# Background steps, a decay clamp and VectorE's order in a two-block network on one Trainium2 core

## The chip, the cores and the metric

The kernel runs on one core of one Trainium2 chip. Its time is the device time in microseconds (us) of one execution. The time before is the median of three runs, 1569.42 us (1568.95 to 1573.41). The engines are TensorE (PE: matmuls, and its weight loads PEld), VectorE (DVE), ScalarE (ACT), GpSimd (POOL) and SyncE (SP), which issues most transfers.

## The reference

Two layers of two blocks work on 256 positions of width 1024. Block 1 adds the output of two mixers, a state-space one (SSD) and a dilated attention, and then a gated feed-forward; block 2 is a retention mixer, a block attention (MoBA) and a gated embedding. Each part begins with an RMS norm. What matters here:

```python
def rms_norm(x, w):
    xf = x.astype(jnp.float32)
    y = xf * lax.rsqrt(jnp.mean(xf * xf, axis=-1, keepdims=True) + RMS_EPS)
    return (y * w.astype(jnp.float32)).astype(x.dtype)
...
def ssd_mixer(z, xbc, dt_raw, conv_w, conv_b, dt_bias, a_log, d_skip, norm_w):
    ...
    dt = jax.nn.softplus(dt_raw.astype(f32) + dt_bias.astype(f32))
    a = -jnp.exp(a_log.astype(f32))
    ...
def ssd_chunked(xh, dt, a, bm, cm):
    ...
    a_cum = jnp.cumsum(a_dt, axis=-1)
    causal = jnp.tril(jnp.ones((SSD_CHUNK, SSD_CHUNK), dtype=bool))
    decay = jnp.exp(jnp.where(causal, a_cum[..., :, None] - a_cum[..., None, :], -jnp.inf))
    cb = jnp.einsum("bclgn,bcsgn->bgcls", cc, bc)
    y_diag = jnp.einsum("bgecls,bcsgep->bclgep", cb[:, :, None] * decay, x)
    decay_states = jnp.exp(a_cum[..., -1:] - a_cum).transpose(0, 3, 4, 1, 2)
```

`dt` are the step sizes, `a_cum` their cumulative sums times a decay rate. The exponent of `decay` is at most 0 below the diagonal; above it the kernel clamps it at 0 and multiplies by a mask later.

## The kernel before

**Weights.** Every large product is made in three passes, high times high, high times low and low times high part. The weights come as 1 MB pieces `raw` on SP's queue; ScalarE casts the high part `wh` (L156), VectorE subtracts it for the low part `wl` (L159), and while `pool_every` is 4 (the bc projections and the SSD groups) GpSimd makes every fourth `wl`. A unit is 128x1024 weights: 24 matmuls with 256 columns (L451 to L453, or L435 to L437), or 12 with 512 (L398 to L400) in the slabs. `split_to` (L143) keeps the casts two units ahead of PE, in three buffers each.

**Background steps.** `tick` (L344) runs once per unit. It advances the first generator of each queue in `self.bg` to its next `yield`. So one `yield` more in a generator puts all that follows in it one unit later. `drain` runs a queue to its end. The queues of `block1` (L704) are `qn` (norm pieces), `qa` (attention), `qs` (SSD groups) and `qt` (group tails).

**Order.** The order of instructions on each engine is set by a scheduler from a timeline of its own, except between `ordered(True)` and `ordered(False)` (L843), where it is the order of the program, for all engines or for those named.

**Block 1.** First the norm and the values of both attention halves, then queries and keys of half 0, queries and keys of half 1 with half 0's `attention` (L498) in the background, then `dt_path` (L546), at once and in one piece, then the bc projections; after the first pair of these, half 1's `attention` goes to `qa`. Each of its four heads takes scores, a softmax (GpSimd adds the three patterns, L526; VectorE scales by L527 and L528), transposes of `E` on PE (L387) and the product with the values.

Then come four groups of 8 heads: the `xs` projection with its convolution (L612 to L617: a ScalarE and three VectorE instructions per tile, then a half-size SiLU, L616 and L617), `z`, and a gate or a branch. `ssd_group` (L619) goes to `qs` at each group's end and runs beside the next group's projections: it loads `abc`, the rows of `a_cum` spread over the partitions (GpSimd's queue), transposes `xs` (L387), and makes in four steps the decay matrices `M`:

```python
nc.vector.tensor_tensor(mb[:, :, 0:3:2, :], abc[...], acum[...], ALU.min)
nc.scalar.activation(m[:, j, 128 * b:128 * b + 128], src, AF.Exp, bias=bias)
nc.gpsimd.tensor_tensor(m, m, cb[:, None, :].to_broadcast([P, 2, 384]), ALU.mult)
```

The clamp is one 128x512 instruction on VectorE (L644), the exponents are six 128x128 activations (L653), with the bias -a_cum (`nacum`) or `rem`. `ssd_tail` (L677) normalizes a group: squares, PE sums (L687), a broadcast (L695), four scalings (L699) and a split into high and low part (L380, L391).

**Slabs.** Where a part begins with a norm, the first products are made before the norm's factors are known: a slab multiplies h times gain, unnormalized, and its results are scaled afterwards. Meanwhile `Norm.steps` (L245) makes the normalized input in four pieces, each two scalings by the broadcast factor (L264), a cast on ScalarE (L380) and a subtraction (L391). In block 1 that is `w_gate_up` with its gating (L821 to L827), in block 2 the projections v and q (L1062 and on); in layer 0 of block 2 `h` itself is scaled as well (L275).

Of the kernel before, what the change touches and what calls it, by code (L numbers as in the profile page):

```python
# [13 lines left out]
AF = mybir.ActivationFunctionType  # L14
# [270 lines left out]
class Net:  # L285
# [212 lines left out]
    def attention(self, v, kT, q0, q1, q2, oh, ol):  # L498
# [4 lines left out]
        for h in range(4):  # L503
# [26 lines left out]
            yield  # L530
            pt = self.transpose4([e[:, 0, 256:384], e[:, 0, 0:128], e[:, 0, 128:256]])
# [12 lines left out]
    def dt_path(self, l, xh, xl, wd):  # L544
# [10 lines left out]
        nc.scalar.copy(raw, ps)  # L555
        pt = self.tr.tile([P, 64], F32, tag="tr", name="tr")
# [3 lines left out]
        def tile2(tag):  # L560
            return self.sp.tile([P, 2, 32], F32, tag=tag, name=tag)
# [9 lines left out]
        nc.vector.tensor_tensor(z2, z, z, ALU.mult)  # L571
        nc.vector.tensor_scalar(q, z2, 1.0 / 15.0, None, op0=ALU.mult)
        for n in (13.0, 11.0, 9.0, 7.0, 5.0, 3.0):
            nc.vector.scalar_tensor_tensor(q, q, 1.0 / n, z2, ALU.add, ALU.mult)
        nc.vector.scalar_tensor_tensor(q, q, 1.0, z, ALU.add, ALU.mult)
        nc.vector.tensor_scalar(x, x, 0.0, None, op0=ALU.max)
# [8 lines left out]
        nc.vector.tensor_scalar(dth, dt, 0.5, None, op0=ALU.mult)  # L585
        pc = self.ch.tile([P, 96], F32, tag="ch", name="ch")
# [5 lines left out]
        nacum = tile2("d_nacum")  # L592
        nc.vector.tensor_scalar(nacum, acum, -1.0, None, op0=ALU.mult)
# [9 lines left out]
        return dth, acum, nacum, rem, scr  # L603
# [15 lines left out]
    def ssd_group(self, l, g, bc, xs, sz, dts, out, tails):  # L619
        nc = self.nc  # L620
        dth, acum, nacum, rem, scr = dts
# [16 lines left out]
        for step in range(6):  # L638
            if step < 4:
                m = ms[step] = self.sp.tile([P, 2, 384], F32, tag="EM", name="M", bufs=3)  # L640
                h0 = 8 * g + 2 * step

                mb = m.rearrange("p j (b c) -> p j b c", b=3)
                nc.vector.tensor_tensor(  # L644
                    mb[:, :, 0:3:2, :], abc[:, 2 * step:2 * step + 2, :].rearrange("p j (b c) -> p j b c", b=2),
                    acum[:, :, h0:h0 + 2].rearrange("p b j -> p j b")[:, :, :, None].to_broadcast([P, 2, 2, P]),
                    ALU.min)
                for j in range(2):
                    hh = h0 + j
                    for b, src, bias in ((0, m[:, j, 0:128], nacum[:, 0, hh:hh + 1]),  # L650
                                         (1, abc[:, 2 * step + j, 128:256], rem[:, hh:hh + 1]),
                                         (2, m[:, j, 256:384], nacum[:, 1, hh:hh + 1])):
                        nc.scalar.activation(m[:, j, 128 * b:128 * b + 128], src, AF.Exp, bias=bias)  # L653
                nc.gpsimd.tensor_tensor(m, m, cb[:, None, :].to_broadcast([P, 2, 384]), ALU.mult)  # L654
# [22 lines left out]
    def ssd_tail(self, l, g, xs, out):  # L677
# [5 lines left out]
        for _ in range(4 if g == 3 else 6):  # L683
            yield
# [18 lines left out]
    def block1(self, l, h, n1):  # L703
# [29 lines left out]
        dts = self.dt_path(l, uh, ul, wd)  # L733
        self.w.pool_every = POOL_EVERY
        bc = self.sp.tile([P, 8, S], F32, tag="big", name="bc")
        for f in range(0, 8, 2):
            ps = self.pairA("w_in", l, C_B + 128 * f, D, getu)
            self.conv_pair(l, ps, 16 + f, bc[:, f:f + 2, :])
            if f == 0:
                self.drain(qa)  # L740
                os.append(self.pair([P, 4, S], "A0", "A1"))
                qa.append(self.attention(*B, *os[1]))
# [59 lines left out]
        self.bg = [[n2.steps()]]  # L802
        acts = []
# [26 lines left out]
        self.drain(self.bg[0])  # L830
        getv = n2.getv
# [231 lines left out]
    def block2(self, l, x, n1):  # L1063
# [7 lines left out]
        def tile(tag, shape, bufs=1):  # L1071
            return sp.tile([P, *shape], F32, tag=tag, name="b2", bufs=bufs)

        qn, qm, qr = [n1.steps()], [], []
        self.bg = [qn, qm, qr]
        mv = tile("B2", [2, 512])
# [5 lines left out]
        self.drain(qn)  # L1082
        getu = n1.getv
# [168 lines left out]
```

## Time and profile before

| | |
|---|---|
| median of three runs | 1569.42 us (1568.95 to 1573.41) |
| profiled execution, its own time | 1576.56 us |
| its span | 1574.8 us |
| PE busy | 1541.3 us, 98% |
| VectorE, ScalarE, GpSimd busy | 74%, 52%, 29% |
| mean granted clock of TensorE | 0.993 |

Busy shares say how much of the span an engine worked. The list of waits and the chain say where another engine held PE up. A row of the timeline has start, duration, engine, line, output and inputs, and in brackets the idle time before it with what ended it.

### The profile page before, as it was taken

Reading aid. Unit: us, or ns where it says so; the run is one execution under the profiler, and the core shown is the slowest. Engines: PE = TensorE matmul, PEld = TensorE weight load, DVE = VectorE, ACT = ScalarE, POOL = GpSimd, SP = SyncE. Lnnn points to the kernel's source line nnn. Section 1 sums busy time; section 2 is a strip of 40 time slices with the busy share of each in tenths; the row PEclk is TensorE's granted clock in tenths of the full one; section 3 lists DMA queues with packets and bytes.
Section 4 is the critical chain, followed back from the end, with each engine's and each line's share of the span. In section 5 each row is a group of like instructions: output and inputs, shape, how many; then the busy total and the mean of one; then the engine's idle time right before and its main releaser. Section 6 shows DMA issues by size and latency. Waiting matters only on the chain.

```text
span 1574.8 us, 29400 instructions
## 1 busy us (share of the span) xinstructions
PE 1541.3 (98%) x12104; PEld 1478.2 (94%) x12104; DVE 1163.3 (74%) x1758; ACT 826.6 (52%) x1276; POOL 462.5 (29%) x285
## 2 busy tenths in 40 slices
PE   9999999989999999999999999999999999999998
PEld 7999999889999999999998999998999979998998
DVE  7888998765577565668897887567655578788776
ACT  6444567545455444544466765445444454456443
POOL 4656356543000000066525565110000112111110
PEclk9999999989999999999999999999999999999999
DMA  8644544445554555554443455455555545455542
GB/s 307 234 167 139 184 162 161 149 146 191 188 182 166 188 187 188 191 210 161 157 166 135 182 193 199 169 203 207 181 184 182 184 159 185 136 188 187 188 147 95
DMA packets 42662, 280.68 MB, mean 178 GB/s; under 512 B 4864, under 2 KB 7040, under 8 KB 10016
## 3 DMA queue, kind: packets, MB, share of 16 engines
q1 hardware_dynamic: 40592, 267.20, 47.9%
q0 software_dynamic: 1936, 11.60, 1.9%
q8 instruction: 95, 1.56, 0.4%
q14 instruction: 39, 0.32, 0.1%
HBM read 274.53 MB, written 4.26 MB: 177 GB/s over the span
## 4 chain that ended last, share of the span: by engine, by line
PE 85%; DVE 8%; ACT 2%; issue 2%; POOL 2%; DMA 1%; DVEq 0%; SPq 0%; POOLq 0%; ACTq 0%
PE mm L451 17%; PE mm L453 17%; PE mm L452 17%; PE mm L435 6%; PE mm L436 6%; PE mm L437 6%; PE mm L399 3%; PE mm L398 3%; PE mm L400 3%; DVE wl L159 2%; PE ch L664 1%; PE tr L387 1%; ACT wh L156 1%; DVE acc L614 1%; DVE E L527 1%
## 5 line engine op out<-in xcount | busy, mean ns | idle before, releaser
L156 ACT CAST wh<-raw 128x1024 fp32r<-128x1024 f32 x488 | 511.0, 1048 | 570.3 <-PE mm L452 381.6
L159 DVE TENSOR_TENSOR wl<-raw,wh 128x1024 fp32r<-128x1024 f32 x456 | 606.1, 1332 | 259.2 <-ACT wh L156 255.7
L453 PE MATMUL mm<-uh,wl 128*128 128x256 f32 x2240 | 629.3, 281 | 5.8 <-DVE wl L159 3.7
L451 PE MATMUL mm<-uh,wh 128*128 128x256 f32 x2240 | 633.2, 283 | 0.1
L452 PE MATMUL mm<-ul,wh 128*128 128x256 f32 x2240 | 627.5, 280 | 0.0
L453 PEld LDWEIGHTS mm<-uh,wl 128*128 128x128 f32 x2240 | 422.9, 189 | 7.3 <-DVE wl L159 4.6
L451 PEld LDWEIGHTS mm<-uh,wh 128*128 128x128 f32 x2240 | 422.6, 189 | 5.1 <-issue 3.5
L452 PEld LDWEIGHTS mm<-ul,wh 128*128 128x128 f32 x2240 | 425.0, 190 | 0.7 <-issue 0.3
L208 POOL TENSOR_TENSOR nsq<-nsq 128x512 f32<-128x512 f32 x19 | 29.7, 1570 | 484.6 <-ACT nsq L202 405.7
L159 POOL TENSOR_TENSOR wl<-raw,wh 128x1024 fp32r<-128x1024 f32 x32 | 79.0, 2470 | 68.2 <-ACT wh L156 63.1
L435 PE MATMUL mm<-A,wh 128*128 128x256 f32 x288 | 82.1, 285 | 1.0 <-ACT wh L156 1.0
L437 PE MATMUL mm<-A,wl 128*128 128x256 f32 x288 | 81.6, 285 | 0.1
L399 PE MATMUL mm<-wl,nu 128*128 128x512 f32 x192 | 77.1, 403 | 2.9 <-DVE wl L159 2.8
L654 POOL TENSOR_TENSOR M<-M,cb 128x768 f32<-128x768 f32 x32 | 69.8, 2197 | 25.7 <-ACT M L653 17.7
L400 PE MATMUL mm<-wh,nu 128*128 128x512 f32 x192 | 76.0, 399 | 0.0
L398 PE MATMUL mm<-wh,nu 128*128 128x512 f32 x192 | 72.6, 401 | 3.0 <-DVE tg L827 2.2
L614 DVE SCALAR_TENSOR_TENSOR acc<-mm,feat,acc 128x255 f32<-128x255 f32 (+1 forms) x144 | 67.2, 475 | 5.1 <-ACT acc L612 3.7
L471 POOL TENSOR_TENSOR qT<-qT,rot 64x512 f32<-64x512 f32 x32 | 56.7, 1773 | 48.5 <-ACT qT L467 48.5
L472 POOL TENSOR_TENSOR qT<-qT,rp 64x512 f32<-64x512 f32 x32 | 60.1, 1877 | 28.3 <-DVE rp L469 28.1
L436 PE MATMUL mm<-A,wh 128*128 128x256 f32 x224 | 63.8, 285 | 0.0
L435 PEld LDWEIGHTS mm<-A,wh 128*128 128x128 f32 x288 | 55.0, 191 | 1.4 <-ACT wh L156 1.3
L437 PEld LDWEIGHTS mm<-A,wl 128*128 128x128 f32 x288 | 54.8, 191 | 0.6 <-DVE wl L159 0.6
(311 smaller groups left out, 2984.3 us busy)
## 6 DMA issues: line engine op xcount, KB each, us to landing
raw<-in_w_dram SPq DMA_DIRECT2D x243, 1024.0 KB, 4.8
abc<-scr POOLq DMA_DIRECT2D x8, 1024.0 KB, 5.3
es<-e POOLq DMA_DIRECT2D x4, 512.0 KB, 4.3
e<-es SPq DMA_DIRECT2D x4, 512.0 KB, 4.5
raw<-in_w_dram SPq DMA_DIRECT2D x2, 512.0 KB, 4.4
h<-in_xT_dram SPq DMA_DIRECT2D x2, 512.0 KB, 9.4
h<-in_xT_dram SPq DMA_DIRECT2D x1, 1024.0 KB, 4.9
hs<-h POOLq DMA_DIRECT2D x1, 1024.0 KB, 5.9
```

Of the source, the lines that this page charges most:

```text
L156: self.nc.scalar.copy(h, raw)
L159: eng.tensor_tensor(lo, raw, h.bitcast(F32), ALU.subtract)
L398: nc.tensor.matmul(ps, xh[:, k0 + k, ts], hw[:, k, :], start=start and k == 0, stop=False)
L399: nc.tensor.matmul(ps, xh[:, k0 + k, ts], lw[:, k, :], start=False, stop=False)
L400: nc.tensor.matmul(ps, xl[:, k0 + k, ts], hw[:, k, :], start=False, stop=stop and k == 1)
L435: nc.tensor.matmul(ps, hw[:, n % 8, :], xh[:, kx, :], start=opens, stop=False)
L436: nc.tensor.matmul(ps, hw[:, n % 8, :], xl[:, kx, :], start=False, stop=False)
L437: nc.tensor.matmul(ps, lw[:, n % 8, :], xh[:, kx, :], start=False, stop=left[f] == 0)
L451: nc.tensor.matmul(ps, hw[:, k, :], xh[:, kx, :], start=j == 0 and k == 0, stop=False)
L452: nc.tensor.matmul(ps, hw[:, k, :], xl[:, kx, :], start=False, stop=False)
L453: nc.tensor.matmul(ps, lw[:, k, :], xh[:, kx, :], start=False, stop=j == n - 1 and k == 7)
L614: nc.vector.scalar_tensor_tensor(acc[:, j, k:S], ps[:, j, 0:S - k], w[:, 3 - k:4 - k], acc[:, j, k:S], ALU.mult, ALU.add)
```

## The change

1. `dt_path` becomes a generator in `qs`, ahead of the first group, with six yields; `nacum` goes.
2. The clamp moves from VectorE to ScalarE. It is Relu(a_cum - abc) on four 128x128 tiles and one Exp with scale -1 over 128x512, beside the two Exp with `rem`: seven activations in a step where there were six, and no VectorE instruction.
3. `attention` waits one step more per head in its second half, `ssd_group` one step at the start of groups 1 and 2, `ssd_tail` seven steps instead of six, group 3 excepted.
4. VectorE runs in program order in the gate_up slabs of block 1 and in the v and q slabs of block 2, in both layers.

```diff
@@ -495,7 +495,7 @@
             out.append(dst)
         return out
 
-    def attention(self, v, kT, q0, q1, q2, oh, ol):
+    def attention(self, v, kT, q0, q1, q2, oh, ol, late=0):
         nc = self.nc
         qs = (q0, q1, q2)
         scale = HD ** -0.5
@@ -528,6 +528,8 @@
             nc.vector.tensor_scalar(e[:, 0, 256:384], e[:, 0, 256:384], mx[:, 3:4], None, op0=ALU.mult)
             yield
             yield
+            for _ in range(late):
+                yield
             pt = self.transpose4([e[:, 0, 256:384], e[:, 0, 0:128], e[:, 0, 128:256]])
             pT = self.sp.tile([P, 384], F32, tag="pT", name="pT", bufs=2)
             nc.scalar.copy(pT, pt[:, 0:384])
@@ -541,7 +543,7 @@
                 self.split(oh[:, h - 1:h + 1, :], ol[:, h - 1:h + 1, :], po)
             yield
 
-    def dt_path(self, l, xh, xl, wd):
+    def dt_path(self, l, xh, xl, wd, out):
 
         nc = self.nc
         ps = self.ch.tile([32, S], F32, tag="ch", name="ch")
@@ -553,6 +555,7 @@
             nc.tensor.matmul(ps, wl[:, cs], xh[:, k, :], start=False, stop=k == 7)
         raw = self.small(S, "qk", QK_BUFS, 32)
         nc.scalar.copy(raw, ps)
+        yield
         pt = self.tr.tile([P, 64], F32, tag="tr", name="tr")
         for t in range(2):
             nc.tensor.transpose(pt[:, 32 * t:32 * t + 32], raw[:, 128 * t:128 * t + 128], self.ident[0:32, 0:32])
@@ -569,10 +572,12 @@
         nc.vector.reciprocal(z, z)
         nc.vector.tensor_tensor(z, z, e, ALU.mult)
         nc.vector.tensor_tensor(z2, z, z, ALU.mult)
+        yield
         nc.vector.tensor_scalar(q, z2, 1.0 / 15.0, None, op0=ALU.mult)
         for n in (13.0, 11.0, 9.0, 7.0, 5.0, 3.0):
             nc.vector.scalar_tensor_tensor(q, q, 1.0 / n, z2, ALU.add, ALU.mult)
         nc.vector.scalar_tensor_tensor(q, q, 1.0, z, ALU.add, ALU.mult)
+        yield
         nc.vector.tensor_scalar(x, x, 0.0, None, op0=ALU.max)
         dt = tile2("d_dt")
         nc.vector.scalar_tensor_tensor(dt, q, 2.0, x, ALU.mult, ALU.add)
@@ -583,14 +588,14 @@
                                        ALU.mult, ALU.mult)
         dth = tile2("d_dth")
         nc.vector.tensor_scalar(dth, dt, 0.5, None, op0=ALU.mult)
+        yield
+        yield
         pc = self.ch.tile([P, 96], F32, tag="ch", name="ch")
         for c in range(2):
             nc.tensor.matmul(pc[:, 32 * c:32 * c + 32], self.tri, adt[:, c, :], start=True, stop=True)
         nc.tensor.matmul(pc[:, 64:96], self.ones, adt[:, 0, :], start=True, stop=True)
         acum = tile2("d_acum")
         nc.vector.tensor_copy(acum, pc[:, 0:64].rearrange("p (c h) -> p c h", c=2))
-        nacum = tile2("d_nacum")
-        nc.vector.tensor_scalar(nacum, acum, -1.0, None, op0=ALU.mult)
         rem = self.small(32, "d_rem", 1)
         nc.vector.tensor_tensor(rem, pc[:, 64:96], acum[:, 0, :], ALU.subtract)
         pr = self.ch.tile([32, S], F32, tag="ch", name="ch")
@@ -600,7 +605,8 @@
         nc.scalar.copy(rows, pr)
         scr = self.dr.tile([32, S], F32, tag="scr", name="scr")
         nc.gpsimd.dma_start(scr, rows)
-        return dth, acum, nacum, rem, scr
+        out.extend((dth, acum, rem, scr))
+        yield
 
     def conv_pair(self, l, ps, ch, dst):
 
@@ -618,7 +624,9 @@
 
     def ssd_group(self, l, g, bc, xs, sz, dts, out, tails):
         nc = self.nc
-        dth, acum, nacum, rem, scr = dts
+        dth, acum, rem, scr = dts
+        if g in (1, 2):
+            yield
         abc = self.sp.tile([P, 8, S], F32, tag="abc", name="abc")
         nc.gpsimd.dma_start(abc, scr[8 * g:8 * g + 8, :].partition_broadcast(P))
         pc = self.ch.tile([P, 384], F32, tag="ch", name="ch")
@@ -641,16 +649,14 @@
                 h0 = 8 * g + 2 * step
 
                 mb = m.rearrange("p j (b c) -> p j b c", b=3)
-                nc.vector.tensor_tensor(
-                    mb[:, :, 0:3:2, :], abc[:, 2 * step:2 * step + 2, :].rearrange("p j (b c) -> p j b c", b=2),
-                    acum[:, :, h0:h0 + 2].rearrange("p b j -> p j b")[:, :, :, None].to_broadcast([P, 2, 2, P]),
-                    ALU.min)
                 for j in range(2):
                     hh = h0 + j
-                    for b, src, bias in ((0, m[:, j, 0:128], nacum[:, 0, hh:hh + 1]),
-                                         (1, abc[:, 2 * step + j, 128:256], rem[:, hh:hh + 1]),
-                                         (2, m[:, j, 256:384], nacum[:, 1, hh:hh + 1])):
-                        nc.scalar.activation(m[:, j, 128 * b:128 * b + 128], src, AF.Exp, bias=bias)
+                    a2 = abc[:, 2 * step + j, :]
+                    for c in range(2):
+                        nc.scalar.activation(mb[:, j, 2 * c, :], a2[:, 128 * c:128 * c + 128], AF.Relu, scale=-1.0,
+                                             bias=acum[:, c, hh:hh + 1])
+                    nc.scalar.activation(mb[:, j, 1, :], a2[:, 128:256], AF.Exp, bias=rem[:, hh:hh + 1])
+                nc.scalar.activation(mb[:, :, 0:3:2, :], mb[:, :, 0:3:2, :], AF.Exp, scale=-1.0)
                 nc.gpsimd.tensor_tensor(m, m, cb[:, None, :].to_broadcast([P, 2, 384]), ALU.mult)
             if step >= 2:
                 pr = step - 2
@@ -680,7 +686,7 @@
         nc.scalar.activation(sq, xs, AF.Square)
         nc.gpsimd.tensor_tensor(sq[:, 0:2, :], sq[:, 0:2, :], sq[:, 2:4, :], ALU.add)
         nc.gpsimd.tensor_tensor(sq[:, 0, :], sq[:, 0, :], sq[:, 1, :], ALU.add)
-        for _ in range(4 if g == 3 else 6):
+        for _ in range(4 if g == 3 else 7):
             yield
         pss = self.ch.tile([P, 2], F32, tag="ch", name="ch")
         for t in range(2):
@@ -730,7 +736,8 @@
         wd = self.pair([P, 256], "acc", "acc", 2)
         self.split(*wd, wraw)
         B = self.qkv_half(l, 1, getu, vs[1])
-        dts = self.dt_path(l, uh, ul, wd)
+        dts = []
+        qs.append(self.dt_path(l, uh, ul, wd, dts))
         self.w.pool_every = POOL_EVERY
         bc = self.sp.tile([P, 8, S], F32, tag="big", name="bc")
         for f in range(0, 8, 2):
@@ -739,7 +746,7 @@
             if f == 0:
                 self.drain(qa)
                 os.append(self.pair([P, 4, S], "A0", "A1"))
-                qa.append(self.attention(*B, *os[1]))
+                qa.append(self.attention(*B, *os[1], 1))
         def halves(tiles):
             return [tiles[f // 4][:, f % 4:f % 4 + 2, :] for f in range(0, 8, 2)]
 
@@ -800,6 +807,7 @@
         n2 = Norm(self, h1, self.gains[:, G_FFN + l, :], EPS1, ("B1", "B2", "u", "u"))
         self.outT("w_out", l, lambda k: (*ms[k // 4], k % 4), self.add_half(h1, n2))
         self.bg = [[n2.steps()]]
+        self.ordered(True, {mybir.EngineType.DVE})
         acts = []
         for th, tl in (("O0", "O1"), ("B3", "B4"), ("A0", "A1"), ("A2", "A3"), ("A4", "B0"), ("B1", "B2")):
             acts.append(self.pair([P, 4, S], th, tl))
@@ -828,6 +836,7 @@
                 us[t] = tg
             qf.append(first_acts(p, us))
         self.drain(self.bg[0])
+        self.ordered(False)
         getv = n2.getv
         for p in range(2, NPAIR):
             pg = self.pairA("w_gate_up", l, 256 * p, D, getv)
@@ -1073,6 +1082,7 @@
 
         qn, qm, qr = [n1.steps()], [], []
         self.bg = [qn, qm, qr]
+        self.ordered(True, {mybir.EngineType.DVE})
         mv = tile("B2", [2, 512])
         self.proj2(l, 6, n1.get, "v", mv, norm=n1)
         if l == 0:
@@ -1080,6 +1090,7 @@
         mq = tile("B0", [4, S])
         self.proj2(l, 4, n1.get, "q", mq, qm, hg[:, 0, :], norm=n1)
         self.drain(qn)
+        self.ordered(False)
         getu = n1.getv
         mk = tile("B1", [4, S])
         self.proj2(l, 5, getu, "k", mk, qm, hg[:, 1, :])
```

PE's order shows part 3 at the head of group 2 in layer 0, where the group's transposes of `xs` (L387) stand among the units: `uh`, `ul`, `A` and `O` are the inputs of projections, `gr` is the factor of group 1's tail. Before:

```order
L452 MATMUL mm<-ul,wh 128x256
L453 MATMUL mm<-uh,wl 128x256
L451 MATMUL mm<-O_1065,wh 128x256
L452 MATMUL mm<-O_1066,wh 128x256
L387 MATMUL tr<-c_80,xs 128x128 x4
L695 MATMUL ch<-c_80,gr 128x128 x2
L387 MATMUL tr<-c_80,xs 128x128 x4
L451 MATMUL mm<-O_1065,wh 128x256
L452 MATMUL mm<-O_1066,wh 128x256
L453 MATMUL mm<-O_1065,wl 128x256
```

The same transposes in the change, the first four:

```order
L452 MATMUL mm<-ul,wh 128x256
L453 MATMUL mm<-uh,wl 128x256
L387 MATMUL tr<-c_80,xs 128x128 x3
L451 MATMUL mm<-uh,wh 128x256
L452 MATMUL mm<-ul,wh 128x256
L387 MATMUL tr<-c_80,xs 128x128
L453 MATMUL mm<-uh,wl 128x256
L451 MATMUL mm<-uh,wh 128x256
```

and the other four:

```order
L452 MATMUL mm<-A_1857,wh 128x256
L453 MATMUL mm<-A_1856,wl 128x256
L387 MATMUL tr<-c_80,xs 128x128 x4
L453 MATMUL mm<-O_1065,wl 128x256
L451 MATMUL mm<-O_1065,wh 128x256
```

The eight stood together around the broadcast L695; now they stand in two places, three units apart, and the broadcast (now L701) comes after both.

VectorE's order shows part 4 at the gate_up slab of layer 0: `nv` is a normalized piece, `ul` its low part, `tg` the gated product. Before:

```order
L372 TENSOR_SCALAR rs_v<-ch 128x2
L159 TENSOR_TENSOR wl<-raw,wh 128x1024
L821 TENSOR_SCALAR nrh<-nr 128x2
L822 TENSOR_TENSOR nrr<-nr 128x2
L159 TENSOR_TENSOR wl<-raw,wh 128x1024
L264 SCALAR_TENSOR_TENSOR nv<-h_4923,gains,ch 128x256 x4
L826 SCALAR_TENSOR_TENSOR tg<-tg,mm 128x256 x2
L391 TENSOR_TENSOR ul<-nv,uh 128x512
L827 SCALAR_TENSOR_TENSOR tg<-tg,nrr,mm 128x256 x2
```

With the change:

```order
L372 TENSOR_SCALAR rs_v<-ch 128x2
L159 TENSOR_TENSOR wl<-raw,wh 128x1024
L264 SCALAR_TENSOR_TENSOR nv<-h_4921,gains,ch 128x256 x2
L391 TENSOR_TENSOR ul<-nv,uh 128x512
L159 TENSOR_TENSOR wl<-raw,wh 128x1024
L264 SCALAR_TENSOR_TENSOR nv<-h_4921,gains,ch 128x256 x2
L391 TENSOR_TENSOR ul<-nv,uh 128x512
L829 TENSOR_SCALAR nrh<-nr 128x2
L830 TENSOR_TENSOR nrr<-nr 128x2
L834 SCALAR_TENSOR_TENSOR tg<-tg,mm 128x256
L835 SCALAR_TENSOR_TENSOR tg<-tg,nrr,mm 128x256
```

Before, two subtractions `wl` came ahead of the first norm piece; now each piece stands whole, scaling and subtraction, between two `wl`, and the gating comes behind two pieces.

## Rows read from the trace of the kernel before

**Rows 1.** The page's parts 1 (busy us, share, xinstructions) and 4 (chain).
```profile
PE 1541.3 (98%) x12104; PEld 1478.2 (94%) x12104; DVE 1163.3 (74%) x1758; ACT 826.6 (52%) x1276; POOL 462.5 (29%) x285
...
PE 85%; DVE 8%; ACT 2%; issue 2%; POOL 2%; DMA 1%; DVEq 0%; SPq 0%; POOLq 0%; ACTq 0%
```

**Rows 2.** PE's list of waits: line waited for: us in total, times, longest.
```profile
PE mm L453 <- DVE wl L159: 8.5, 5, 2.4
PE tr L387 <- DVE E L528: 4.6, 5, 1.9
...
PE tr L387 <- DVE xs L617: 1.5, 2, 0.7
...
PE tr L387 <- DVE mx L518: 0.7, 1, 0.7
```

**Rows 3.** Windows: length, busy (xcount) PE PEld DVE ACT POOL, PEclk, DMA, GB/s.
```profile
490.00:600.00 110.00, 110.00 (x935) 110.00 (x934) 65.04 (x67) 49.73 (x58) 0.00 (x0) 1.00 0.53 190
348.00:354.00 6.00, 6.00 (x28) 6.00 (x29) 4.40 (x8) 1.04 (x1) 0.00 (x0) 0.50 0.46 167
845.00:850.00 5.00, 5.00 (x30) 4.12 (x27) 3.82 (x6) 3.81 (x13) 1.47 (x1) 0.66 0.22 54
1282.00:1287.00 5.00, 4.75 (x14) 3.76 (x15) 3.84 (x6) 2.07 (x11) 0.72 (x1) 0.66 0.79 236
330.00:334.00 4.00, 4.00 (x24) 4.00 (x23) 3.24 (x4) 3.48 (x5) 2.75 (x2) 0.57 0.15 25
300.00:303.00 3.00, 3.00 (x16) 3.00 (x16) 3.00 (x5) 1.05 (x1) 0.00 (x0) 0.50 0.62 262
```

**Rows 4.** PE's timeline, heads of groups 2 and 3: start, us, instruction [idle before].
```profile
295.49 0.66 PE L387 MATMUL tr<-c,xs 128*128 128x128 f32 x4 [0.75 <-DVE xs L617]
...
298.78 0.39 PE L453 MATMUL mm<-O,wl 128*128 128x256 f32 x1 [2.40 <-DVE wl L159]
...
329.12 0.39 PE L453 MATMUL mm<-uh,wl 128*128 128x256 f32 x1 [1.94 <-POOL wl L159]
```

**Rows 5.** PE's timeline, second attention half of layer 1.
```profile
817.37 0.39 PE L453 MATMUL mm<-uh,wl 128*128 128x256 f32 x1 [1.33 <-DVE wl L159]
```

**Rows 6.** Groups by line: xcount | busy us, mean ns | idle before, releasers.
```profile
L644 DVE TENSOR_TENSOR M<-abc,d_acum 128x512 f32<-128x512 f32 x32 | 29.6, 936 | 17.2 <-DMA abc<-scr 13.3 <-PE ch L664 3.2 <-PE tr L387 0.7
...
L616 ACT ACTIVATE xs<-acc 128x512 f32<-128x512 f32 x16 | 10.1, 632 | 6.7 <-DVE acc L614 6.5
```

**Rows 7.** ScalarE's timeline, a step of SSD group 1.
```profile
272.49 1.28 ACT L653 ACTIVATE M<-abc,d_rem 128x128 f32<-128x128 f32 x4 [0.37 <-DMA abc<-scr]
```

**Rows 8.** One line's instructions, L527: duration ns min/median/max.
```profile
L527 DVE TENSOR_SCALAR E<-E,mx x16: 339/1367/2470, 105.9 to 865.2; 128x256 f32<-128x256 f32 x16
```

**Rows 9.** Timeline of GpSimd and VectorE, first transposes of E in layer 0.
```profile
185.60 2.37 POOL L159 TENSOR_TENSOR wl<-raw,wh 128x1024 fp32r<-128x1024 f32 x1
...
185.67 2.45 DVE L527 TENSOR_SCALAR E<-E,mx 128x256 f32<-128x256 f32 x1 [0.51 <-POOL E L526]
```

**Rows 10.** PE's timeline, the dt path of layer 1.
```profile
787.63 0.63 PE L588 MATMUL ch<-d_adt,c 128*128 128x32 f32 x4 [0.96 <-DVE d_adt L582]
```

**Rows 11.** VectorE's timeline, the gate_up slab of layer 0.
```profile
470.77 1.23 DVE L159 TENSOR_TENSOR wl<-raw,wh 128x1024 fp32r<-128x1024 f32 x1 [1.86 <-ACT wh L156]
471.91 1.65 DVE L264 SCALAR_TENSOR_TENSOR nv<-h,gains,ch 128x256 f32<-128x256 f32 x4
...
474.14 0.68 DVE L391 TENSOR_TENSOR ul<-nv,uh 128x512 fp32r<-128x512 f32 x1
```

**Rows 12.** ScalarE's and PE's timeline, the gate_up slab of layer 0.
```profile
472.81 0.62 ACT L380 CAST uh<-nv 128x512 fp32r<-128x512 f32 x1 [1.34 <-DVE nv L264]
...
475.36 0.47 PE L398 MATMUL mm<-wh,nu 128*128 128x512 f32 x1 [1.08 <-DVE tg L827]
```

**Rows 13.** VectorE's and PE's timeline, first slabs of block 2, layer 0.
```profile
1276.64 1.26 DVE L275 SCALAR_TENSOR_TENSOR h<-h,gains,ch 128x256 f32<-128x256 f32 x3
...
1282.26 0.50 PE L399 MATMUL mm<-wl,nu 128*128 128x512 f32 x1 [2.08 <-DVE wl L159]
```

## The prediction

> **What bounds the kernel now.** I read the page's busy shares and chain first: TensorE (PE) is busy for 1541.3 of 1574.8 us and is 85% of the chain of work that ended last [rows 1]. So an operation taken off VectorE or put on ScalarE counts only where PE waits for it. At full clock PE retires 935 matmuls in 110 us [rows 3], 8.5 per us, so a weight unit of 24 matmuls lasts 2.82 us. That is the beat by which VectorE and ScalarE must have the next unit's `wl` and `wh` ready.
>
> Then PE's list of waits [rows 2]. Over all 1574.8 us only some 20 us of waiting bears on this change, and the timeline shows where: at the head of the SSD groups [rows 4], in the second attention half [rows 5], at the dt path [rows 10], in the two kinds of norm slab [rows 12, 13].
>
> A wait costs twice when it is long. Behind the waits of 2.40, 1.94, 2.40, 1.9 and 2.08 us (at 298, 329, 347, 844 and 1282 us) the granted clock falls to the lower of its two levels (1.2 instead of 2.4 GHz): the windows that follow have a mean of 0.50, 0.57, 0.50, 0.66 and 0.66, with 16, 24, 28, 30 and 14 matmuls where full clock would do 25.5, 34, 51, 42.5 and 42.5 (the 14 have 512 columns and count as 28) [rows 3]. The matmuls missing, divided by 8.5, are 1.1, 1.2, 2.7, 1.5 and 1.7 us. Behind the shorter waits I count nothing.
>
> **Heads of groups 2 and 3, layer 0.** At 295.49 the transposes of `xs` wait 0.75 us for L617, and three matmuls later the next `wl` is 2.40 us late, since L617 and that subtraction lie one behind the other on VectorE; at 329.12 a `wl` made by GpSimd is 1.94 us late [rows 4]. The first pair stands once more at 344.68 and 347.96 with the same sizes (L617 has 1.5 us in two waits [rows 2]). Together 0.75 + 2.40 + 1.94 + 0.75 + 2.40 = 8.2 us, and the clock behind them 1.1 + 1.2 + 2.7 = 5.0. The extra yield of groups 1 and 2 and of the tails parts the transposes from the tail's broadcast, the `min` (32 x 936 ns [rows 6]) leaves VectorE, and the eight transposes, together before, now stand in two places three units apart. I take all 13.2 us as gone.
>
> What is late next is a cast: ScalarE now has seven activations in a step, and a `wh` cast stands behind them. Four back-to-back 128x128 activations end 1.28 us after the first begins [rows 7], 0.31 each; six of them (1.9) and a 128x512 one (0.63 [rows 6]) make 2.5, and with a 1.05 cast 3.55 us, 0.7 over PE's beat. In two places per group that is 4 x 0.7 = 2.8 back. **Gain 13.2 - 2.8 = 10.4.**
>
> **The clamp on ScalarE.** Six activations a step were 1.9 us, seven are 2.5: 32 x 0.6 = 19 us more ScalarE. It has room (826.6 us busy [rows 1]), so it costs where a cast is due behind it. Bounds: 0, and all 19. The other six groups have no wait at their heads now, so I let one cast in three of the 0.7 kind show in each, 6 x 0.25 = **1.5 lost**; nearer to 0, because the three M buffers let ScalarE run ahead. A rule of the Trainium skill speaks against this part: "ScalarE: Activation LUTs", section "Rules for kernel authors", sends relu, max and min to VectorE rather than ScalarE; by it the clamp should have stayed, and if ScalarE were the bound the sum would end near the third rival's time. The rows agree on the length (four 0.31 us activations are longer than 0.94 us), not that it decides.
>
> **Second attention half.** The transposes of E wait 4.6 us in all for L528, the longest 1.9 [rows 2]. With 0.7 for `mx` [rows 2] and the `wl` at 817.37 that comes 1.33 late [rows 5], and 1.5 of clock behind the 1.9, there are 4.6 + 0.7 + 1.3 + 1.5 = 8.1 us. One more yield gives a unit, 2.82 us, more than the longest wait. But L527 is 339 ns at its shortest and 2470 at its longest, median 1367 [rows 8]: at 185.67 it began 0.07 us after a GpSimd subtraction and ended 0.15 after it [rows 9], so it can be later still where GpSimd moves too. The Trainium skill's "SBUF — State Buffer", section "Who interferes with whom", has VectorE and GpSimd share a port pair that one instruction holds whole; the pair of rows agrees, and by it the fourth rival gains weight. I take two thirds of 8.1: **gain 5.4** (bounds 0 and 8.1).
>
> **The dt path.** The wait of 0.96 for `d_adt` [rows 10] goes, because the two yields put PE's cumulative sums two units later. In layer 1, though, the transposes of E then fall among the 24 small dt matmuls, about 1.3 us sooner after L528; I add 1.4. **Cost 0.4.** Dropping `nacum`, one small VectorE instruction per layer, and the two SP issues that move are hidden: no wait in the list names either. The store of `scr` on GpSimd's queue comes six steps later, and group 0's `abc` is loaded behind it; between them lie the bc, xs and z projections, 16 units of 2.82 us, which cover it.
>
> **Program order on VectorE in the norm slabs.** Now `wl` is issued where the program has it, behind a whole norm piece. A piece is two L264 (1.65 / 4 each), the cast `uh` on ScalarE (0.62), then `ul` (0.68): 0.83 + 0.62 + 0.68 = 2.13 us, during which VectorE sits on a semaphore; before, a `wl` or four L264 filled that time [rows 11, 12]. With the 1.23 subtraction a round trip is 3.36 against PE's 2.82.
> - The two gate_up slabs: the second unit's `wl` is 2.1 late. The gate's products L834 and L835, for which PE waited 1.08 at 475.36 [rows 12], now stand behind the second piece, 2.1 late as well. 2.13 + 2.13 - 1.08 = 3.2, twice: **6.4 lost**. No clock is counted in the likeliest case; both waits are near the size that cost some.
> - Block 2, layer 1: six units of v and q, each 3.36 - 2.82 = 0.54 over: **3.2 lost**; little waits there now.
> - Block 2, layer 0: the same 3.2, and the scaling of `h` (L275, 1.26 for three [rows 13]) puts two more, 0.84, ahead of one `wl`: 4.0. Gone are 2.08 [rows 13] and 1.7 of clock: **0.2 lost**.
> Together 9.8. Bounds: 0 (PE has two units in hand), and with a clock fall in each slab, below.
>
> **Sum.** -10.4 + 1.5 - 5.4 + 0.4 + 9.8 = -4.1 us against the profiled execution of 1576.56, which stands 7.14 above the median of the runs, 1569.42. So 1572.5 as profiled, **1565.3 as a median**.
>
> **Rivals.**
> 1. Slower: the slabs' waits pull the clock down. Place: the four slabs. Price: two waits of over 2 us in each gate_up slab and a sum of 3 to 4 in the others; if each slab draws one stretch as dear as the window at 348, 4 x 2.7 = 10.7 more. It decides once the slabs cost more than the 13.9 gained elsewhere. For: every wait of 1.9 or more in this trace was followed by a fall. Against: the others' waits are split into halves of a us. -4.1 + 10.7 = +6.6: 1576.0.
> 2. Faster: program order costs nothing, because PE works off the units in hand, and only the gains stand: -4.1 - 9.8 = -13.9: 1555.5. With the leftover casts too, -18: 1551. For: the subtraction at 470.77 now has 1.86 us of idle time ahead of it [rows 11]. Against: that idle time is spent waiting for ScalarE's cast.
> 3. ScalarE becomes the bound in the eight groups, and the whole 19 shows: 19 - 1.5 = 17.5 more, -4.1 + 17.5 = +13.4: 1582.8. Against: it is busy 52% [rows 1].
> 4. The later steps don't do what they are for: the transposes of E still find GpSimd ahead of L528 and half the groups' waits return: -4.1 + 5.4 + 5.2 = +6.5, less about 2 of clock that the shorter of these waits spare: +4.5, 1573.9. For: the spread of L527 [rows 8].
>
> **How the numbers follow.** Chances: forecast 0.38, first rival 0.20, second 0.28, third 0.04, fourth 0.10. 0.3%, 4.7 us, is about what a measurement can tell from no change: below 1564.7 is faster, above 1574.1 slower. The forecast's own range is 1560 to 1571, of which a third is faster; the second rival is faster; the first and third are slower but for a small part; of the fourth half. Faster 0.13 + 0.28 = 0.41; slower 0.17 + 0.04 + 0.05 = 0.26; same 0.33. The range 1552 to 1579 holds the forecast, nearly all of rivals 1, 2 and 4, and leaves out the third and the extremes.
>
> **What would show it.** Right: no PE wait for L623 (the former L617) and full clock from 299 to 361; E waits under 2 us in all; in the slabs new PE waits for `wl` of 2 us in layer 0's gate_up, six of half a us in block 2. Wrong: no new wait in the slabs (second rival), a clock of 0.5 there (first), PE waits for `wh` casts in all eight groups (third), unchanged waits of the E transposes (fourth).

## The result and the profile after

The changed kernel takes 1589.49 us (median, 1586.34 to 1590.78) against 1571.0: a ratio of 1.0114, interval 1.0091 to 1.0138, so some 18 us slower. The forecast was 1565.3, the range 1552 to 1579; the measured time lies above it.

The page's busy line of the changed kernel, then PE's list of waits, to be held against [rows 1, 2] (L623 is the former L617, L835 the former L827):

```profile
PE 1542.2 (97%) x12104; PEld 1473.2 (93%) x12104; DVE 1138.2 (72%) x1724; ACT 842.1 (53%) x1308; POOL 468.6 (30%) x285
```

```profile
PE mm L399 <- DVE wl L159: 9.3, 12, 2.1
PE mm L453 <- DVE wl L159: 8.7, 8, 2.5
PE tr L387 <- DVE E L528: 4.9, 4, 2.1
PE mm L398 <- DVE tg L835: 4.0, 2, 2.1
PE mm L451 <- DVE rs_v L372: 3.2, 2, 1.6
PE tr L387 <- DVE xs L623: 2.2, 3, 1.5
```

VectorE has 25 us less to do and ScalarE 15.5 more, yet the sums of the waits that were to go are no smaller: E 4.9, `xs` 2.2, `wl` 8.7 in the 256-column units. They stand at other places, though. At the heads of groups 2 and 3 in layer 0 the 2.40 us for `wl` are now 1.0, followed by 1.6 put down to L372, and new are 1.84 for E and 1.46 for `xs`, one behind the other, at 253 and 255 us, and 2.47 for `wl` at 882. In the slabs `wl` costs 9.3 (2.8 before) and the gating 4.0 (2.2 before).

Where the time lies shows by a landmark that all versions share: the start of the k-th weight cast (L156) on ScalarE. The table gives, for stretches between two casts, the length in a version's profiled execution minus that in the kernel before's.

| stretch (casts) | change | e1 | e2 | e7 | e8 | e10 | e12 | e13 |
|---|---|---|---|---|---|---|---|---|
| start, same program (0 to 44) | -1.4 | -0.1 | -1.3 | +5.4 | -1.5 | +5.9 | -1.2 | -1.4 |
| attention, groups, layer 0 (44 to 112) | -3.3 | -0.3 | -5.2 | -4.8 | -7.1 | -17.7 | -8.4 | -15.3 |
| gate_up slab, layer 0 (130 to 146) | +6.2 | 0 | +6.2 | +1.4 | -0.3 | -0.3 | 0 | -0.3 |
| attention, groups, layer 1 (230 to 310) | +3.3 | +3.2 | 0 | +0.1 | -5.2 | +0.4 | +7.0 | +3.2 |
| gate_up slab, layer 1 (330 to 340) | +4.2 | -0.3 | +3.1 | +2.1 | 0 | 0 | -0.3 | -0.3 |
| slabs of block 2, layer 0 (390 to 420) | -0.1 | -1.0 | -0.1 | -1.2 | -0.5 | -0.6 | -0.3 | -0.4 |
| slabs of block 2, layer 1 (440 to 460) | +3.7 | -0.3 | +3.7 | +2.2 | 0 | -0.5 | -0.4 | -0.3 |

For the change, the four slabs lose 14.0 us, and the stretches where 16 us were to be gained end level. The versions e1 to e13 follow below.

A column is one execution, and that of the kernel before wasn't typical in the second row. There the order of instructions on all four engines is the same in e2 and e7 as in the kernel before, and yet they take 5.2 and 4.8 us less. The heads of groups 2 and 3, kernel before, then e2:

```profile
293.00:361.00 68.00, 59.65 (x448) 56.17 (x447) 46.99 (x58) 31.69 (x54) 31.34 (x16) 0.90 0.39 140
```

```profile
292.00:360.00 68.00, 61.18 (x492) 57.64 (x491) 52.05 (x63) 34.07 (x59) 34.55 (x18) 0.95 0.44 158
```

e2 makes 44 matmuls more. The wait of 1.94 us at 329 [rows 4] doesn't come in it, and the lower clock is granted for about 7 us there, for 14 in the kernel before. So in the second row a version is better held against -5 than against 0: the change and e1, which have the same order there too, lose 2 and 5 us, e8 gains 2, e12 3, e13 10 and e10 13.

PE's timeline in the slab at 464 us of the changed kernel, then VectorE's:

```profile
469.33 0.50 PE L399 MATMUL mm<-wl,nu 128*128 128x512 f32 x1 [2.08 <-DVE wl L159]
...
473.14 0.77 PE L398 MATMUL mm<-wh,nu 128*128 128x512 f32 x1 [1.87 <-DVE tg L835]
...
474.14 0.63 PE L400 MATMUL mm<-wh,nu 128*128 128x512 f32 x1
474.56 0.63 PE L398 MATMUL mm<-wh,nu 128*128 128x512 f32 x1
...
477.71 0.39 PE L400 MATMUL mm<-wh,nu 128*128 128x512 f32 x1
477.94 0.40 PE L398 MATMUL mm<-wh,nu 128*128 128x512 f32 x1
```

```profile
465.89 0.87 DVE L264 SCALAR_TENSOR_TENSOR nv<-h,gains,ch 128x256 f32<-128x256 f32 x2 [1.80 <-PE ch L225]
467.45 0.69 DVE L391 TENSOR_TENSOR ul<-nv,uh 128x512 fp32r<-128x512 f32 x1 [0.69 <-ACT uh L380]
468.06 1.22 DVE L159 TENSOR_TENSOR wl<-raw,wh 128x1024 fp32r<-128x1024 f32 x1
```

VectorE scales a piece, idles 0.69 us for ScalarE's cast, subtracts, and only then makes the `wl` for which PE waits 2.08. Behind the second wait nine matmuls come every 0.42 us or so instead of every 0.23, some 2 us in all. The granted clock there:

```profile
473.00:477.00 4.00, 3.85 (x9) 3.11 (x10) 2.73 (x5) 0.86 (x1) 0.00 (x0) 0.50 0.09 37
```

Without part 4 a `wl` or a gating product stands in VectorE's gap [rows 11]. In layer 1's slab the same two waits, 2.08 and 2.14 us, go by without a fall:

```profile
1089.00:1095.00 6.00, 3.80 (x15) 2.85 (x16) 4.76 (x12) 1.87 (x4) 0.00 (x0) 1.00 0.50 175
```

### The profile page after: what moved, and what is told of

The parts are those of the page before. It is cut to its first block, busy times and chain, and to the rows that moved or that the text cites. A ratio compares the mean times of both kernels' runs of the same rounds, so it can differ in the third digit from the quotient of the medians.

```text
span 1587.8 us, 29368 instructions
## 1 busy us (share of the span) xinstructions
PE 1542.2 (97%) x12104; PEld 1473.2 (93%) x12104; DVE 1138.2 (72%) x1724; ACT 842.1 (53%) x1308; POOL 468.6 (30%) x285
## 5 line engine op out<-in xcount | busy, mean ns | idle before, releaser
L156 ACT CAST wh<-raw 128x1024 fp32r<-128x1024 f32 x488 | 511.2, 1049 | 590.5 <-PE mm L452 391.2
L660 POOL TENSOR_TENSOR M<-M,cb 128x768 f32<-128x768 f32 x32 | 69.2, 2175 | 41.6 <-DVE mx L518 17.5
L472 POOL TENSOR_TENSOR qT<-qT,rp 64x512 f32<-64x512 f32 x32 | 65.0, 2031 | 28.3 <-DVE rp L469 28.2
```

Source lines behind the costliest of these rows:

```text
L156: self.nc.scalar.copy(h, raw)
```

## The experiments

Medians in us; "over" and "under" are differences of the ratio to the kernel before, taken times 1570.

**First, the parts.** e1 is the change without the four `ordered` lines, e2 the kernel before with these alone:

```diff
+        self.ordered(True, {mybir.EngineType.DVE})
...
+        self.ordered(False)
```

> The change without part 4 (the scheduler orders VectorE in the slabs again). Theory S: the slabs' program order is the whole slowdown, and parts 1 to 3 together are worth about nothing, since in the change's trace PE's lost time from 186 to 400 us fell by only 2 to 3 us. Then this run stands within 4 us of the kernel before, some 14 to 18 us under the change. Rival P: parts 1 to 3 have made it slower by themselves (casts behind the longer ScalarE chains, moved transposes), and the slabs give part of their waits back later; then it stands 6 us or more over the kernel before. The forecast's own sum for parts 1 to 3 alone was 14 us under it.

> The kernel before with part 4 alone. Theory S: the gate_up slabs show the two waits of 2.1 and 1.9 us that the change's trace has at 469.33 and 473.14, and block 2 of layer 1 loses about 4: in all 11 to 16 us over the kernel before. Rival P: no more than 6 over it. Block 2 of layer 0 should stay about level, by both.

e1: 1574.95, ratio 1.0033 (1.0021 to 1.0045), 5 over. e2: 1579.9, 1.0068 (1.0050 to 1.0086), 11 over. Together 16 of the change's 18. The slabs are the larger share, but e1 lies between theory S (within 4) and rival P (6 or more): parts 1 to 3 are not worth nothing, they cost 5.

e3 is part 2 alone, e4 part 3 alone, each the hunks shown above with the change.

> The kernel before with part 2 alone (the clamp as Relu on ScalarE). Theory S: 4 us under to 4 us over the kernel before; the long VectorE instructions beside GpSimd's M products (L617 at 2 us, wl at 2.5 to 3.4) stay, so PE's waits at the heads of the groups stay. Rival P: 6 us or more over it, with PE waits for wh casts.

> The kernel before with part 3 alone (one yield more per head, in groups 1 and 2, and in the tails). Theory S: 5 us under to 2 us over the kernel before, waits moved and not removed. Rival P: 4 us or more over it. The forecast: 8 or more under it, the waits of E and of the heads of groups 2 and 3 gone.

e3: 1571.94, 1.0015 (1.0000 to 1.0030). e4: 1572.4, 1.0015 (0.9997 to 1.0032). Each is some 2 over, with an interval that touches no change, and neither is the gain of the forecast. PE's waits in e3, then in e4:

```profile
PE mm L453 <- DVE wl L159: 4.6, 5, 1.3
PE ch L685 <- POOL sq L680: 2.7, 2, 1.4
PE ch L662 <- DVE xdt L632: 1.8, 1, 1.8
```

```profile
PE tr L387 <- DVE E L528: 7.9, 5, 4.8
PE mm L453 <- POOL wl L159: 6.3, 5, 1.6
```

In e3 the waits for `wl` fall from 8.5 [rows 2] to 4.6, and others come that the kernel before doesn't have. In e4 the E transposes, which were to be a step late enough, wait longer: 7.9 for 4.6. The longest, 4.81, is for an L528 that takes 5.91 us instead of 0.27 and ends 0.1 after a row of GpSimd's instructions; VectorE, then the last of GpSimd's:

```profile
236.65 5.91 DVE L528 TENSOR_SCALAR E<-E,mx 128x128 f32<-128x128 f32 x1
```

```profile
240.14 2.33 POOL L159 TENSOR_TENSOR wl<-raw,wh 128x1024 fp32r<-128x1024 f32 x1
```

**Second, the mechanisms.** e5 shortens GpSimd's product in the kernel before, leaving out two thirds of it, and e6 does so in e1:

```diff
-                nc.gpsimd.tensor_tensor(m, m, cb[:, None, :].to_broadcast([P, 2, 384]), ALU.mult)
+                nc.gpsimd.tensor_tensor(m[:, :, 0:128], m[:, :, 0:128],
+                                        cb[:, None, 0:128].to_broadcast([P, 2, 128]), ALU.mult)
```

> The kernel before, with GpSimd's product of M and the mask made on the first 128 of each 384 columns only, so that two thirds of it are left out (the output is not the reference's). Theory V: at the heads of the SSD groups VectorE is the bound, because its instructions take two to three times their length beside GpSimd's 2.2 us products (L617 2.33 instead of 0.68, wl 3.37 instead of 1.22). Then L617 and wl come back to 0.7 and 1.2 there, the waits of 8.2 us at the heads of groups 2 and 3 shrink to under 4, and the time falls by 6 to 14 us. Rival O: the order of the instructions sets the waits, GpSimd only fills the time: less than 4 us.

> Parts 1 to 3 without program order, with the same shortened M product. Theory V: this falls by 6 to 14 us against parts 1 to 3 with the full product and ends within 4 us of the kernel before with the short product: what parts 1 to 3 were to take away was VectorE's stretched time, which they only shift. Rival O: it stays 5 us or more over that run, the moved order being dear by itself.

e5: 1553.21, 0.9893 (0.9866 to 0.9921), 17 under, more than expected. e6: 1557.2, 0.9918 (0.9892 to 0.9944), 13 under, 18 under e1 and 4 over e5, at the edge of theory V. By line, the kernel before and e5:

```profile
L654 POOL TENSOR_TENSOR M<-M,cb 128x768 f32<-128x768 f32 x32 | 69.8, 2197 | 25.7 <-ACT M L653 17.7 <-DVE cb L628 6.7 <-issue 1.2
...
L617 DVE SCALAR_TENSOR_TENSOR xs<-xs,acc 128x512 f32<-128x512 f32 x16 | 17.4, 1085 | 0.1
```

```profile
L654 POOL TENSOR_TENSOR M<-M,cb 128x256 f32<-128x256 f32 x32 | 29.1, 925 | 29.2 <-ACT M L653 14.9 <-DVE cb L628 9.6 <-DVE wl L159 4.4
...
L617 DVE SCALAR_TENSOR_TENSOR xs<-xs,acc 128x512 f32<-128x512 f32 x16 | 12.1, 756 | 0.1
```

The edit touches GpSimd alone, and VectorE's L617 falls from 1085 to 756 ns. Shorter products also let the scheduler choose another order, in layer 0's groups above all, so the 17 us need not be the overlap alone. In layer 1 (casts 230 to 310) the order on all four engines is the kernel before's, and there VectorE's 387 instructions take 239 us in sum instead of 249, the 1.87 us for E at 844 and the clock fall behind them are gone, and the stretch is 3.5 us shorter: that part is the overlap. L617 isn't the measure of it in every order: in e6 (as L623) it still takes 1120 ns on average.

e7 is e2 with each piece's subtraction one background step later:

```diff
-            net.split(self.vh[:, f:f + 2, :], self.vl[:, f:f + 2, :], v)
+            nc.scalar.copy(self.vh[:, f:f + 2, :], v)
             if f < 6:
                 yield
+            net.low(self.vl[:, f:f + 2, :], v, self.vh[:, f:f + 2, :])
```

> The kernel before with part 4, but each norm piece's subtraction is written one background step after its cast, so that VectorE in program order has a wl and never sits on the ScalarE cast between a piece's scaling and its subtraction. Theory R (the round trip VectorE, ScalarE, VectorE is the slabs' price): the 2.1 us wait for the second wl falls to about 0.8, the gating's 2.1 to about 1.1, the six half-microsecond waits of block 2 to under 0.3; 0 to 5 us over the kernel before, where part 4 alone was 10 over. Rival W: any program order puts wl too late; 8 us or more over.

e7: 1573.6, 1.0026 (1.0006 to 1.0046), 4 over where e2 was 11 over. PE's timeline in its slab:

```profile
473.41 0.50 PE L400 MATMUL mm<-wl,nu 128*128 128x512 f32 x1 [0.70 <-DVE wl L159]
...
476.89 0.47 PE L399 MATMUL mm<-wh,nu 128*128 128x512 f32 x1 [1.80 <-DVE tg L829]
```

The `wl` wait fell from 2.08 to 0.70, as the round trip demands; the gating's only to 1.80, where 1.1 was expected. In the table the gate_up slabs of layer 0 and 1 fall from 6.2 and 3.1 to 1.4 and 2.1, and some 2 us of the first are the clock, which doesn't fall in e7. In block 2 theory R fails: the waits that were to be under 0.3 stay at about 0.5 and more, and with part 4 layer 1 has one of 1.4 for GpSimd's `nr`, in e7 as in e2. So the round trip is the larger part of the gate_up slabs' price and little of block 2's.

e8 is part 1 alone.

> The kernel before with part 1 alone (the step sizes as background steps; the negated sums are kept). Theory V: 2 us under to 4 us over; the wait for d_adt goes, the transposes of E in layer 1 wait up to 2 us more. The forecast had 0.4 over. Rival O: 4 us or more over.

e8: 1563.79, 0.9952 (0.9937 to 0.9968), 7.5 under: a gain that neither theory had. The second attention half of layer 1, before and in e8:

```profile
812.00:860.00 48.00, 43.89 (x336) 40.86 (x335) 38.81 (x85) 28.52 (x59) 22.79 (x14) 0.96 0.39 138
```

```profile
812.00:860.00 48.00, 48.00 (x402) 45.93 (x401) 41.30 (x76) 35.78 (x79) 28.98 (x19) 1.00 0.44 157
```

PE runs through, without the waits at 817, 834 and 844 us. The half comes earlier in e8, its first transposes 2 us behind the last of the step sizes' VectorE instructions instead of 22, and the scalings L527 of its second and third head, 2.45 and 1.89 us before, take 0.34 and 0.35: they no longer meet a long instruction of GpSimd's. The second head before, VectorE and GpSimd, then VectorE in e8:

```profile
832.36 2.45 DVE L527 TENSOR_SCALAR E<-E,mx 128x256 f32<-128x256 f32 x1 [0.64 <-POOL E L526]
...
832.28 2.37 POOL L159 TENSOR_TENSOR wl<-raw,wh 128x1024 fp32r<-128x1024 f32 x1
```

```profile
815.81 0.34 DVE L527 TENSOR_SCALAR E<-E,mx 128x256 f32<-128x256 f32 x1
```

That this is what lets PE run through wasn't tried by itself.

**Third, on top of part 1.** e9 adds the attention's later step, e10 those of groups and tails, e11 the clamp.

> Part 1 and the attention half's later step. Part 1 alone was 6.6 us under the kernel before; parts 1 to 3 together 5.3 over, so parts 2 and 3 cost some 12 on top of it. Theory C (collision): one step more per head puts the transposes of E of layer 0's last head beside group 1's transposes of xs, where parts 1 to 3 have waits of 1.8 and 1.6 us one behind the other and a clock fall. Then this loses 4 to 9 of part 1's gain, and the wait stands at about 254 us. Rival G: the groups' and tails' later steps are what costs; then this stays within 2 us of part 1 alone.

> Part 1 and the later steps of groups and tails. Theory C: 0 to 5 us over part 1 alone, most of it in layer 1's groups 2 and 3 (part 3 on the kernel before lost 6 to 7 there). Rival G: 7 us or more over part 1 alone.

> Part 1 and the clamp on ScalarE (this is also part 2 without the later steps). Theory C: 0 to 5 us over part 1 alone: the clamp on the kernel before was 2.3 over, 5 of it in layer 1's groups 2 and 3 against less in layer 0. Rival A (the clamp gains once the step sizes are out of the way): 2 us or more under part 1 alone.

e9: 1573.29, 1.0008 (0.9992 to 1.0024), 9 over e8, as theory C has it, but not at its place: at 254 us nothing waits, and layer 1's groups lose instead, with 1.59 us for GpSimd's squares at 905. e10: 1557.63, 0.9906 (0.9882 to 0.9930), 15 under the kernel before and 7 under e8. Both theories had a loss there and both fall. e11: 1567.13, 0.9981 (0.9965 to 0.9998), 4.5 over e8, as expected.

e10 beats both kernels. Groups 1 to 3 of layer 0, before (some 5 us of the difference are that one execution) and in e10:

```profile
262.00:362.00 100.00, 91.65 (x720) 86.33 (x719) 71.72 (x92) 54.42 (x99) 51.57 (x28) 0.93 0.43 158
```

```profile
262.00:362.00 100.00, 100.00 (x851) 94.52 (x851) 76.44 (x105) 60.51 (x108) 62.97 (x32) 1.00 0.53 192
```

**Fourth, what takes it back.** e12 is e10 with the clamp on ScalarE, e13 is e10 with the attention's later step.

> Part 1, the later steps of groups and tails, and the clamp on ScalarE. Part 1 with the later groups was 12.8 us under the kernel before, parts 1 to 3 were 5.3 over: 20 us lie between, of which the clamp on part 1 alone cost 3 to 5 and the attention's later step on part 1 alone 6 to 9. Theory K (the two costs add): this is 3 to 6 us over part 1 with the later groups, about 9 under the kernel before. Rival L (the clamp undoes what the later groups gave, since its longer ScalarE chain puts wh casts and sq behind it at the heads of the groups): 9 us or more over part 1 with the later groups.

> Part 1 and all the later steps, with the clamp on VectorE. Theory K: 6 to 10 us over part 1 with the later groups, 3 to 7 under the kernel before. Theory M (the attention's later step and the groups' are at odds, since both move work to the heads of the groups): 14 us or more over part 1 with the later groups, at the time of the kernel before or over it.

e12: 1573.46, 1.0019 (1.0004 to 1.0034), 18 over e10: rival L's size. e13: 1562.32, 0.9951 (0.9937 to 0.9966), 7 over e10, as theory K. Timelines of e12 in layer 1, of PE, VectorE and GpSimd:

```profile
908.96 0.55 PE L451 MATMUL mm<-O,wh 128*128 128x256 f32 x1 [6.07 <-DVE sz L774]
```

```profile
902.50 5.72 DVE L159 TENSOR_TENSOR wl<-raw,wh 128x1024 fp32r<-128x1024 f32 x2
908.14 0.68 DVE L774 SCALAR_TENSOR_TENSOR sz<-sz,mm 128x512 f32<-128x512 f32 x1
```

```profile
899.78 4.07 POOL L660 TENSOR_TENSOR M<-M,cb 128x768 f32<-128x768 f32 x2 [0.58 <-DVE cb L636]
903.82 3.31 POOL L159 TENSOR_TENSOR wl<-raw,wh 128x1024 fp32r<-128x1024 f32 x1
```

PE waits 6.07 us for L774, which takes a finished product out of PE's accumulator and stands behind two `wl` of 2.86 us each instead of 1.23, beside the end of the second M product, a `wl` of GpSimd's and its squares. In the changed kernel the same pattern stands at the heads of groups 2 and 3 (the wait put down to L372 ends with it, but three convolution steps and the second stretched `wl` stand ahead of L372); PE, VectorE and GpSimd there:

```profile
294.82 0.39 PE L453 MATMUL mm<-uh,wl 128*128 128x256 f32 x1 [1.01 <-DVE wl L159]
...
299.82 0.49 PE L451 MATMUL mm<-O,wh 128*128 128x256 f32 x1 [1.65 <-DVE rs_v L372]
```

```profile
290.00 1.97 DVE L623 SCALAR_TENSOR_TENSOR xs<-xs,acc 128x512 f32<-128x512 f32 x1
...
292.28 2.48 DVE L159 TENSOR_TENSOR wl<-raw,wh 128x1024 fp32r<-128x1024 f32 x1
...
295.67 2.57 DVE L159 TENSOR_TENSOR wl<-raw,wh 128x1024 fp32r<-128x1024 f32 x1
```

```profile
288.64 5.04 POOL L660 TENSOR_TENSOR M<-M,cb 128x768 f32<-128x768 f32 x2 [0.56 <-DVE cb L636]
...
297.12 3.33 POOL L159 TENSOR_TENSOR wl<-raw,wh 128x1024 fp32r<-128x1024 f32 x1
```

**Fifth, ScalarE or GpSimd.** e14 is e12, e15 is e10, both with the short product.

> Part 1, the later groups and the clamp on ScalarE, with GpSimd's product of M made on the first 128 of each 384 columns only (two thirds of it left out, the output is not the reference's). The clamp cost 16 us on top of part 1 with the later groups; the trace shows one PE wait of 6.07 us at 908.96 behind two wl that take 5.72 us beside GpSimd's products. Theory V2 (the clamp's price is this overlap of VectorE with GpSimd, which the min on VectorE had kept apart): with the short product the clamp costs 0 to 5 us, and this run ends within 5 us of its partner without the clamp. Rival L2 (the price is ScalarE's longer chain, casts and sq behind it): the clamp costs 9 us or more with the short product too.

> The partner: part 1 and the later groups with the clamp on VectorE and the same short product (two thirds of the product left out). Both theories: 0 to 8 us under the same kernel with the full product, since few waits at the heads of the groups are left there; 1550 to 1558 us.

e14: 1554.64, 0.9898 (0.9882 to 0.9914). e15: 1553.3, 0.9887 (0.9868 to 0.9906). With short products the clamp costs 2 us, not 18, though ScalarE's chain is as long as in e12. So its price hangs on GpSimd's products and not on ScalarE's chain alone. Nor is it, in the main, another order that the scheduler picks for shorter products: in the two rows of attention and groups VectorE's order in e14 is e12's but for some 20 of 695 instructions, and they take 9.4 and 8.4 us less (a part of it clock); in e15 it is e10's but for 4 of 727, and they take 0.4 and 4.8 less. What stays argued is why VectorE meets GpSimd more in e12's order than in e10's.

## Why the prediction was wrong

- **Slabs: right in mechanism, near in size.** Forecast 6.4 for the two gate_up slabs without clock, 3.2 and 0.2 in block 2, 9.8 in all. Measured 6.2 + 4.2, 3.7 and -0.1, 14.0 in all. In the gate_up slabs the two waits came as worked out, 2.08 and 1.87 for 2.1 and 2.1; what was missing is the first rival in part, some 2 us for a fall of the clock in layer 0, and 1 us in layer 1 without a fall. e7 shows the round trip to be the larger part of the cause there. Block 2's sizes are luck: in layer 1 there are 1.5 us in three waits for `wl` instead of six of half a us, and 1.4 for GpSimd's `nr`, which I hadn't reckoned. That every wait of 1.9 or more is followed by a fall, the first rival's argument, doesn't hold: 2.08 and 2.14 us in layer 1 were not.
- **Heads of groups: the step that failed is "I take all 13.2 us as gone".** In the change the whole stretch is only 3.3 us shorter. Some 5 of the 13.2 belonged to the one execution that I read: with the same order of instructions e2 and e7 have neither the wait of 1.94 nor the fall behind it, and only half of the fall at 348. The waits of 0.75 and 2.40 and the fall at 300 come again in them, so those were the program's. They went in e10, 13 us against e2 and e7, but the clamp on ScalarE brings 9.3 back in layer 0 and 6.7 in layer 1 (e12 against e10). The attention's later step adds 2.4 in layer 0 without the clamp (e13), and 5 to 8 with it: then E and `xs` wait one behind the other at 253 us, as in the change.
- **Clamp: mis-sized, 1.5 for 2 to 18.** I counted the `min` leaving VectorE as relief and looked for the price at ScalarE's casts. It hangs on GpSimd's products: 2 alone (e3, with an interval from 0 to 5), 4.5 on part 1 (e11), 18 on e10 (e12), 2 with short products (e14, e15). The third rival had the size, 17.5 more, and the wrong engine. The Trainium skill's rule that a relu belongs on VectorE ("ScalarE: Activation LUTs", "Rules for kernel authors") would have kept e10's gain; no run here shows its reason, the speed per element, to be the one that counts.
- **Second attention half: forecast 5.4 gained, measured 7 to 9 lost** (e9 against e8, e13 against e10). Part 1 had taken the gain already, and the fourth rival's mechanism, E still behind GpSimd, is seen in e4: 7.9 us of waits, with an L528 of 5.91 us. The port pair that "SBUF — State Buffer" of the Trainium skill describes in "Who interferes with whom" agrees with [rows 9], with that L528 and with layer 1 of e5.
- **Step sizes: forecast 0.4 lost, measured 7.5 gained.** The E wait in layer 1 came about as forecast (2.1 in e8, 0.3 before), and `d_adt` still waits 0.5, as it does in e7 without part 1; but the later waits of the second half, which I had booked to part 3, went with part 1.
- **The base.** 1576.56 stood 7.1 above the median, and I subtracted that as a constant. The medians of five later sets of runs of the kernel before are 1569.6 to 1570.8, with single runs up to 1579. Since e2 and e7 take some 5 us less in the second row of the table with the same order of instructions, most of the offset was, it seems, the same time that I booked as gain.

Parts 1 and 3's groups together were the forecast's core, 10.4 - 0.4 = 10 gained; e10 gives 15. That it is near is partly luck: 7.5 of the 15 are part 1's, for which I had forecast a loss.

## What to carry to other kernels

VectorE's instructions took up to some 20 times their length beside GpSimd's here (5.91 us for 0.27 in e4), so ask of every step that is moved what will then run beside what. That the `min` had paced GpSimd fits e12, but isn't shown by itself. Program order on one engine is dear where a piece goes out to another engine and back; write the return a step later. And before a clock loss in one profile is booked as a gain, see whether another execution of the same code has it.

## What the runs showed of the hardware

Some clock falls come and go with the same program, others come again. The start of the kernel, the same in all versions, took 5 to 6 us more in e7 and e10 (and in e3 and e4) than in the others: PE waited 2.8 us for `gr` at 46 us, and the granted clock fell twice. e10, then e8:

```profile
20.00:60.00 40.00, 36.39 (x173) 30.51 (x174) 29.89 (x40) 21.48 (x28) 22.34 (x13) 0.87 0.60 216
```

```profile
20.00:60.00 40.00, 38.16 (x225) 32.59 (x225) 36.36 (x53) 25.10 (x32) 23.78 (x17) 1.00 0.68 254
```

Of the falls in the kernel before up to 850 us, those at 300, 348 and 845 stand in e2 and e7 as well, with the same order of instructions; that at 330 doesn't.

In the feed-forward, with the same order of matmuls and the full clock, PE's pace differs between executions; the kernel before, then e2:

```profile
540.00:580.00 40.00, 40.00 (x342) 40.00 (x342) 24.11 (x25) 18.66 (x22) 0.00 (x0) 1.00 0.51 185
```

```profile
540.00:580.00 40.00, 40.00 (x356) 40.00 (x355) 24.45 (x27) 19.32 (x22) 0.00 (x0) 1.00 0.56 203
```

40 us hold 342 or 356 matmuls, 117 or 112 ns each; e2 has the quicker pace in both layers, e7 in the second alone. The cause is open.
